# Layer 1's stick-breaking attention written out in slots of one head, and running sums of two convolutions held in PSUM

## The chip, the cores and the metric

The kernel runs on one core of a Trainium2 chip. The metric is the device time of one execution in microseconds (us). Of the kernel before there are three runs, 2133.7, 2135.2 and 2140.45 us; their median is 2135.2. A separate execution was profiled: it took 2129.01 us, of which 2127.0 us are the span that the trace covers.

## The reference

256 tokens of 1024 channels pass a first block (four mixers side by side, an output projection, an MLP) and a second block of two layers (a pooling layer and a stick-breaking attention, each followed by a PEER layer of 16384 experts). All is float32. What the change touches:

```python
def conformer_conv_mixer(u, dw_w, dw_b, gn_g, gn_b):          # 31 taps a channel
    val, gate = jnp.split(u, 2, axis=-1)
    z = val * jax.nn.sigmoid(gate)
    z = causal_depthwise_conv(z, dw_w) + dw_b
    z = group_norm_channels(z, gn_g, gn_b)
    return jax.nn.silu(z)

def rglru_mixer(u, conv_w, conv_b, wa, ba, wx, bx, lam):      # 4 taps a channel
    xr, gate = jnp.split(u, 2, axis=-1)
    xc = causal_depthwise_conv(xr, conv_w) + conv_b
    ...
    _, h = lax.associative_scan(combine, (a, bterm), axis=1)
    return (h * jax.nn.gelu(gate.astype(jnp.float32))).astype(u.dtype)

# second block, layer 1: 16 heads of 64 channels, 16 meta tokens in front of 256
q = rmsnorm(jnp.einsum('bld,de->ble', hn, w_q[j]).reshape(B, L, SB_HEADS, SB_HEAD_DIM), q_norm[j])
mix = jnp.einsum('ble,ed->bld', stick_breaking(q, k_sh, v_sh), w_o[j])
# in stick_breaking, by blocks of 128 queries
    z = jnp.einsum('bhqd,bhkd->bhqk', q_blk, kp) * scale
    valid = (key_pos[None, :] < q_pos[:, None]) & key_real[None, :]
    log_keep = jnp.where(valid, jax.nn.log_sigmoid(-z), 0.0)
    after = lax.cumsum(log_keep, axis=3, reverse=True) - log_keep
    wgt = jnp.where(valid, jnp.exp(jax.nn.log_sigmoid(z) + after), 0.0)
    return jnp.einsum('bhqk,bhkd->bqhd', wgt.astype(v.dtype), vp)
```

## The kernel before, in words

Channels lie on the 128 partitions and tokens along them, 256 tokens in the first block and 272 (L, with the meta tokens, NM = 16) in the second. Weights come as tiles of 128 x 1024 float32 through four raw buffers that SyncE's queue fills (`_Stream`). Each tile is split in two: ScalarE copies it in the reduced format to one of three `hi` buffers (line 256), and VectorE or GpSimd subtracts to get `lo` (line 267); the letters in the tables from line 357 on ("V" or "G") say which. `proj` (line 424) multiplies one tile with the activations, 16 products with `hi` (activations high and low in turn) and 8 with `lo`; `acc3` does the same for the output projections, with the sums of all 8 output tiles in four banks. PSUM has eight banks `bank[0]` to `bank[7]`. Every instruction that goes through the wrappers `T` (TensorE), `V` (VectorE), `S` (ScalarE) and `G` (GpSimd, mostly) has the line 200 in the trace, so groups are told apart by tile names and shapes; `big` is the large SBUF tile from which most work arrays are cut.

The mixers. The 20 tiles of the input projection follow one another in the order `W_ORD`. Behind each, the generators of the mixers are pulled: `conf(0)`, the 31-tap convolution of the first 128 channels, on VectorE; `conf(1)`, the second 128, with products on ScalarE and additions on GpSimd; `lru()`, the recurrent mixer, whose four taps, elementwise work and scans run on VectorE, ScalarE and GpSimd; and `att(c)`, softmax attention of 4 heads. A pull hands out an allowance in ns for each engine, from which each step takes what it yields (335 for a tap of `conf(0)`). The output projection then takes the mixers' rows in the order `K_ORD` = 4, 6, 2, 5, 7, 3, 1, 0, where 6 and 7 are the recurrent mixer's; its inputs are split into `XX` on ScalarE and VectorE. In both stages the program text is only the starting point: outside blocks under `tc.manual_schedule()` a scheduler reorders the instructions of each engine by its own model of the time.

A tap multiplies a shifted input with one weight per partition and adds the running sum, one VectorE instruction of 128 x 256:

```python
V.scalar_tensor_tensor(acc, zp[c][:, t:t + SEQ], cols[:, w0 + t:w0 + t + 1], acc, op0=ALU.mult, op1=ALU.add)
```

The attention of layer 1 (`stick`). First the 8 blocks of values are projected and turned to tokens on partitions (`v_out`), in three pieces of keys, 0 to 127, 128 to 255, and 256 to 271. `project(c)` projects one K tile and one Q tile, each holding two heads, squares them, sums the squares over a head by a product with ones (`half`), and takes the norm: for K by Ln and Exp on ScalarE, for Q by an addition on VectorE, a power on GpSimd (line 1652) and a multiplication by 0.125. `attend(c)` does two heads: scores of the first 128 queries against 144 keys and of the other 128 against 272, VectorE adds the mask, ScalarE takes Abs, Exp and Ln, VectorE adds the maximum and runs two reversed scans, GpSimd subtracts (line 1675), ScalarE takes Exp. The weights are turned by five transposes, copied to SBUF by ScalarE and VectorE, and multiplied by the values with the turned weights as TensorE's stationary operand and 64 columns of values moving; the result of two heads is copied, transposed twice, and split into `aH` and `aL`. In the text `project(c + 1)` stands ahead of `attend(c)`, and the output projection with `wo` behind all heads; the scheduler mixes them.

## Time and profile before

| | |
|---|---|
| median of three runs | 2135.2 us (2133.7 to 2140.45) |
| profiled execution, its span | 2129.01 us, 2127.0 us |
| TensorE matmuls busy | 2048.0 us, 96% of the span |
| VectorE busy | 1619.5 us, 76% |
| ScalarE busy | 1264.3 us, 59% |
| GpSimd busy | 1095.2 us, 51% |
| mean granted clock of TensorE | 0.972 |

The span is the time between the first and the last instruction in the trace, and a share is busy time by span. TensorE counts as busy while a matmul is in it, also where it runs at a lower clock, so its 96% doesn't say that it worked at full speed. The granted clock is 1.0 at 2.4 GHz and 0.5 at 1.2 GHz, and a mean between them is a mixture. In time, the input projection and the mixers lie before 131.5 us, then the MLP, the pooling layer, the first PEER layer, from 1168.84 us on the attention of layer 1, and behind it the second PEER layer.

### The profile page before, as it was taken

To read this page: it belongs to the slowest core of one execution; us is meant where nothing else is said; L and a number is where in the kernel's file an instruction comes from. 1 tells how busy PE (TensorE), PEld (TensorE's weight loads), DVE (VectorE), ACT (ScalarE), POOL (GpSimd) and SP (SyncE) were. 2 spreads that over 40 slices of the span, in tenths; PEclk is the share of its full clock that TensorE was granted. 3 is DMA by queue.
4 is the path that set the end of the run, shared out by engine and by line. 5 is a ranking of instruction groups with operands and counts; after the bars stand their busy time and mean duration, and the time that the engine had idled before them with its cause. 6 is when DMAs were issued, how large, how long until landed. Compare 5 with 4: busy or idle time off the path is not lost.

```text
span 2127.0 us, 42088 instructions
## 1 busy us (share of the span) xinstructions
PE 2048.0 (96%) x15922; PEld 1960.2 (92%) x15924; DVE 1619.5 (76%) x3169; ACT 1264.3 (59%) x2541; POOL 1095.2 (51%) x671
## 2 busy tenths in 40 slices
PE   7889999999999998999999999899999998999999
PEld 6789998999999996999999988899999997999998
DVE  7964845999688788788887484899766677877875
ACT  4654445555777785555555574455688876555554
POOL 5745836587677772333332351568776763333200
PEclk8999999999999997999999997999999998999999
DMA  5336653355676775899895521445676666889874
GB/s 187 129 111 205 210 191 102 123 190 185 207 239 210 256 239 196 312 332 345 309 316 201 164 85 54 156 135 189 197 238 218 210 209 210 309 297 330 306 251 140
DMA packets 127962, 451.54 MB, mean 212 GB/s; under 512 B 16576, under 2 KB 19776, under 8 KB 126992
## 3 DMA queue, kind: packets, MB, share of 16 engines
q1 hardware_dynamic: 100192, 352.86, 49.6%
q0 software_dynamic: 24592, 88.32, 11.3%
q10 hardware_dynamic: 2976, 7.68, 1.0%
q8 instruction: 126, 2.06, 0.4%
q14 instruction: 76, 0.62, 0.1%
HBM read 445.00 MB, written 3.67 MB: 211 GB/s over the span
## 4 chain that ended last, share of the span: by engine, by line
PE 69%; DVE 13%; issue 4%; ACT 4%; POOL 3%; DMA 1%; POOLq 0%; ACTq 0%; DVEq 0%
PE bank L200 69%; DVE big L200 9%; POOL lo L267 2%; ACT hi L256 1%; ACT oHL L200 1%; DVE bank L200 1%; DVE lo L267 1%; DVE XX L200 1%; DVE oAB L200 1%; POOL big L1257 1%; ACT big L200 1%; DMA big<-ur,sp_e 0%; DMA raw<-u 0%; DVE lo L200 0%; POOL big L943 0%
## 5 line engine op out<-in xcount | busy, mean ns | idle before, releaser
L200 PE MATMUL bank<-XX,hi 128*128 128x224 f32 (+3 forms) x7360 | 1135.0, 303 | 21.4 <-ACT hi L256 9.3
L200 PEld LDWEIGHTS bank<-XX,hi 128*128 128x128 f32 x7360 | 1001.5, 192 | 52.7 <-ACT hi L256 12.0
L256 ACT ACTIVATE hi<-raw 128x1024 fp32r<-128x1024 f32 x616 | 649.4, 1056 | 401.1 <-PE bank L200 372.5
L267 POOL TENSOR_TENSOR lo<-raw,hi 128x1024 fp32r<-128x1024 f32 x276 | 675.1, 2460 | 379.1 <-ACT hi L256 329.5
L200 PE MATMUL bank<-XX,lo 128*128 128x224 f32 (+2 forms) x4672 | 630.0, 276 | 7.2 <-POOL lo L267 5.7
L200 PEld LDWEIGHTS bank<-XX,lo 128*128 128x128 f32 x4672 | 595.0, 192 | 17.3 <-POOL lo L267 8.2
L267 DVE TENSOR_TENSOR lo<-raw,hi 128x1024 fp32r<-128x1024 f32 x340 | 433.0, 1274 | 163.8 <-ACT hi L256 144.8
L200 ACT ACTIVATE big<-bank 128x256 f32<-128x256 f32 (+33 forms) x391 | 125.1, 325 | 152.0 <-DVE big L200 79.6
L200 ACT ACTIVATE oHL<-oAB,picks 128x128 f16<-128x128 f16 x592 | 189.7, 389 | 13.3 <-DVE oAB L200 13.3
L200 DVE TENSOR_TENSOR big<-big,bank 128x256 f32<-128x256 f32 (+38 forms) x295 | 91.8, 312 | 122.1 <-ACT big L200 112.1
L200 DVE SCALAR_TENSOR_TENSOR big<-big 128x1024 f32<-128x1024 f32 (+5 forms) x89 | 117.2, 1321 | 17.9 <-DMA big<-ur,sp_e 9.1
L1257 POOL DMA_INDIRECT big<-v,sp_e x48 | 68.7, 1431 | 106.5 <-DVE big L200 103.5
L1257 POOL DMA_INDIRECT big<-ur,sp_e x56 | 79.2, 1415 | 85.7 <-DVE big L200 81.2
L200 DVE TENSOR_TENSOR oAB<-bank,picks 128x1024 f16<-128x1024 f32 (+1 forms) x112 | 114.2, 1034 | 0.0
L200 PE MATMUL bank<-big 128*128 128x128 f32 (+9 forms) x472 | 88.1, 315 | 11.4 <-ACT big L200 8.7
L200 ACT ACTIVATE XX<-big 128x224 fp32r<-128x224 f32 (+1 forms) x216 | 81.4, 377 | 28.0 <-DVE big L200 27.8
L200 PE MATMUL bank<-oHL,oAB 128*128 128x128 f16 x896 | 79.5, 226 | 15.0 <-ACT oHL L200 11.2
L200 PEld LDWEIGHTS bank<-big 128*128 128x128 f32 (+3 forms) x472 | 67.5, 197 | 24.3 <-ACT big L200 11.1
L200 DVE TENSOR_TENSOR XX<-big,XX 128x224 fp32r<-128x224 f32 (+1 forms) x214 | 86.1, 404 | 0.0
L256 ACT ACTIVATE hi<-more 128x1024 fp32r<-128x1024 f32 x48 | 50.9, 1060 | 56.8 <-PE bank L200 55.3
L200 PEld LDWEIGHTS <-oAB 128*128 128x128 f16 x896 | 55.6, 100 | 28.4 <-issue 20.9
L200 ACT ACTIVATE big<-big 128x416 f32<-128x416 f32 (+5 forms) x120 | 53.8, 469 | 45.4 <-DVE big L200 36.9
(189 smaller groups left out, 2383.3 us busy)
## 6 DMA issues: line engine op xcount, KB each, us to landing
raw<-u SPq DMA_DIRECT2D x256, 512.0 KB
raw<-v SPq DMA_DIRECT2D x208, 512.0 KB
raw<-w SPq DMA_DIRECT2D x64, 512.0 KB
more<-v SPq DMA_DIRECT2D x48, 512.0 KB
raw<-wq SPq DMA_DIRECT2D x32, 512.0 KB
raw<-win SPq DMA_DIRECT2D x16, 512.0 KB
raw<-wkv SPq DMA_DIRECT2D x16, 512.0 KB
raw<-wout SPq DMA_DIRECT2D x8, 512.0 KB
```

The costliest lines, as they stand in the source:

```text
L200: i = f(*a, **k)
L256: nc.scalar.activation(hi, raw, AF.Copy)
L267: eng.tensor_sub(self.lo[i % self.nh], raw, self.hi[i % self.nh].bitcast(F32))
L1257: nc.gpsimd.indirect_dma_start(out=dst, out_offset=None, in_=src, in_offset=bass.IndirectOffsetOnAxis(ap=at, axis=0))
```

## The change

In the mixers the running sum of `conf(0)` is kept in `bank[1]` and that of the four taps of `lru` in `bank[7]`; the last tap of each writes to SBUF. A tap of `conf(0)` now yields 400 instead of 335.

In the attention the values come in two pieces of 128 keys (the 256 tokens) and one of 16 (the meta tokens); the head's output is computed already transposed, with 64 columns of values as the stationary operand and the turned weights moving; the factor 0.125 is folded into the norm of the keys. Everything from the values on is written out in one order under `tc.manual_schedule()`: slots from -3 to 17, one head each, where the scores are of head s, the transposes of head s - 1 and the outputs of head s - 2, with one K or Q tile in each slot up to 12 and the `wo` tiles in slots 13 to 17. `mid` is the product with ones, placed between the products with `hi` and those with `lo`. The remaining helpers (`k_in`, `k_norm`, `k_out`, `q_in`, `q_norm`, `z_in`, `z_act`, `z_scan`, `z_exp`) hold the same instructions as the text before.

```diff
@@ -371,8 +371,8 @@
         for b in range(8):
             st.add(A["wkv"][8 + b], "A", "GVVVVGVV"[b])
         for b in range(8):
-            st.add(A["wkv"][b], "A", "GVVVGVVV"[b])
-            st.add(A["wsq"][b], "A", "GVVGGGGG"[b])
+            st.add(A["wkv"][b], "A", "V")
+            st.add(A["wsq"][b], "A", "G")
         for b in range(8):
             st.add(A["wo"][b], "A", "V")
         add_peer(1)
@@ -421,11 +421,12 @@
             T.matmul(out, xl, wh, start=False, stop=False)
             T.matmul(out, xh, wl, start=False, stop=last)
-        def proj(out, wt, xh, xl):
+        def proj(out, wt, xh, xl, mid=lambda: None):
             h, l = wt
             for k in range(KC):
                 T.matmul(out, h[:, k], xh[:, k], start=k == 0, stop=False)
                 T.matmul(out, h[:, k], xl[:, k], start=False, stop=False)
+            mid()
             for k in range(KC):
                 T.matmul(out, l[:, k], xh[:, k], start=False, stop=k == KC - 1)
@@ -572,11 +573,12 @@
                 w0 = COLS["conf_dw_w"] + 31 * c
                 acc = new()
                 if c == 0:
-                    V.tensor_scalar(acc, zp[c][:, 0:SEQ], cols[:, w0:w0 + 1], C("conf_dw_b", c), op0=ALU.mult, op1=ALU.add)
-                    yield (335, 0, 0)
+                    pacc = bank[1][:, 0:SEQ]
+                    V.tensor_scalar(pacc, zp[c][:, 0:SEQ], cols[:, w0:w0 + 1], C("conf_dw_b", c), op0=ALU.mult, op1=ALU.add)
+                    yield (400, 0, 0)
                     for t in range(1, 31):
-                        V.scalar_tensor_tensor(acc, zp[c][:, t:t + SEQ], cols[:, w0 + t:w0 + t + 1], acc, op0=ALU.mult, op1=ALU.add)
-                        yield (335, 0, 0)
+                        V.scalar_tensor_tensor(acc if t == 30 else pacc, zp[c][:, t:t + SEQ], cols[:, w0 + t:w0 + t + 1], pacc, op0=ALU.mult, op1=ALU.add)
+                        yield (400, 0, 0)
                 else:
                     tmp = [new() for _ in range(3)]
                     S.activation(acc, zp[c][:, 0:SEQ], AF.Identity, scale=cols[:, w0:w0 + 1], bias=C("conf_dw_b", c))
@@ -616,9 +618,10 @@
                 xc, r, ig, tau, rec, a, m = (new(2, SEQ) for _ in range(7))
                 for c in range(2):
                     w0 = COLS["lru_conv_w"] + 4 * c
-                    V.tensor_scalar(xc[:, c], xrp[c][:, 0:SEQ], cols[:, w0:w0 + 1], C("lru_conv_b", c), op0=ALU.mult, op1=ALU.add)
+                    px = bank[7][:, 0:SEQ]
+                    V.tensor_scalar(px, xrp[c][:, 0:SEQ], cols[:, w0:w0 + 1], C("lru_conv_b", c), op0=ALU.mult, op1=ALU.add)
                     for t in range(1, 4):
-                        V.scalar_tensor_tensor(xc[:, c], xrp[c][:, t:t + SEQ], cols[:, w0 + t:w0 + t + 1], xc[:, c], op0=ALU.mult, op1=ALU.add)
+                        V.scalar_tensor_tensor(xc[:, c] if t == 3 else px, xrp[c][:, t:t + SEQ], cols[:, w0 + t:w0 + t + 1], px, op0=ALU.mult, op1=ALU.add)
                         yield (400, 0, 0)
                 for c in range(2):
                     bk = bank[7]
...
-                V.tensor_scalar_mul(m[:, 16:20], m[:, 16:20], 0.125)
...
-                    T.transpose(tbk[:, 0:128], a[:, 0:128], ident)
-                    T.transpose(tbk[:, 128:256], a[:, 144:272], ident)
-                    T.transpose(tbk[:, 256:384], a[:, 272:400], ident)
-                    T.transpose(t2k[0:16, 0:128], a[:, 128:144], ident)
-                    T.transpose(t2k[0:16, 128:256], a[:, 400:416], ident)
-                    S.activation(w[:, 0:384], tbk[:, 0:384], AF.Copy)
-                    V.tensor_copy(w[0:16, 384:640], t2k[0:16, 0:256])
-                    hs = slice(64 * h, 64 * h + 64)
-                    o = [obk[:, 128 * i + 64 * hh:128 * i + 64 * hh + 64] for i in range(2)]
-                    T.matmul(o[0], w[:, 0:128], vt[0][:, hs], start=True, stop=False)
-                    T.matmul(o[0], w[0:16, 384:512], vt[1][0:16, hs], start=False, stop=True)
-                    T.matmul(o[1], w[:, 128:256], vt[0][:, hs], start=True, stop=False)
-                    T.matmul(o[1], w[:, 256:384], vt[1][:, hs], start=False, stop=False)
-                    T.matmul(o[1], w[0:16, 512:640], vt[2][0:16, hs], start=False, stop=True)
-                at = atok[c % 2]
-                S.activation(at, obk[:, 0:256], AF.Copy)
-                for i in range(2):
-                    T.transpose(obk[:, 256 + 128 * i:384 + 128 * i], at[:, 128 * i:128 * i + 128], ident)
-                S.activation(aH[:, c], obk[:, 256:512], AF.Copy)
-                V.tensor_sub(aL[:, c], obk[:, 256:512], aH[:, c].bitcast(F32))
...
-            project(0)
-            for c in range(8):
-                    project(c + 1)
-                attend(c)
-            for c in range(8):
-                h, l = st.get(1 if c == 7 else None)
...
+            def v_copy(b):
+                bk = bank[2 + b % 2]
+                S.activation(vt[:, :, 128 * b:128 * b + 128], bk[:, 0:256].rearrange("p (j d) -> p j d", j=2), AF.Copy)
+                S.activation(va[0:16, 128 * b:128 * b + 128], bk[0:16, 256:384], AF.Copy)
...
+                        V.scalar_tensor_tensor(kq, C("k_norm"), 0.125, C("q_norm"), op0=ALU.mult, op1=ALU.mult)
...
+            def k_tile(c, mid):
+                proj(kbank(c), st.get(1), XH, XL, mid)
...
+            def turn(h):
+                a = ab[h % 4]
+                T.transpose(bank[1][:, 0:128], a[:, 16:144], ident)
+                T.transpose(bank[1][:, 128:256], a[:, 160:288], ident)
+                T.transpose(bank[1][:, 256:384], a[:, 288:416], ident)
+                T.transpose(bank[2][0:16, 0:128], a[:, 0:16], ident)
+                T.transpose(bank[2][0:16, 128:256], a[:, 144:160], ident)
+            def w_copy(h):
+                w = wt_[h % 4]
+                S.activation(w[:, 0:384], bank[1][:, 0:384], AF.Copy)
+                V.tensor_copy(w[0:16, 384:640], bank[2][0:16, 0:256])
+            def o_mm(h):
+                w = wt_[h % 4]
+                o = bank[3][64 * (h % 2):64 * (h % 2) + 64, 0:256]
+                hs = slice(64 * h, 64 * h + 64)
+                T.matmul(o, vt[:, 0, hs], w[:, 0:256], start=True, stop=False)
+                T.matmul(o[:, 128:256], vt[:, 1, hs], w[:, 256:384], start=False, stop=False)
+                T.matmul(o, va[0:16, hs], w[0:16, 384:640], start=False, stop=True)
+            def o_out(c):
+                S.activation(aH[:, c], bank[3][:, 0:256], AF.Copy)
+                V.tensor_sub(aL[:, c], bank[3][:, 0:256], aH[:, c].bitcast(F32))
...
+                for s in range(-3, 18):
+                    live = 0 <= s < 16
+                    for i in {-3: (4, 5), -2: (6, 7)}.get(s, ()):
+                        v_copy(i)
+                    for i in (6, 7) if s == -3 else ():
+                        v_mul(i)
+                    if 0 <= s - 2 < 16:
+                        w_copy(s - 2)
+                    kc = (s + 2) // 2 if s % 2 == 0 and s < 13 else None
+                    qc = kd = (s + 1) // 2 if s % 2 and 0 < s + 1 < 15 or s == -1 else None
+                    mid = lambda: None
+                    if kc is not None:
+                        k_in(kc)
+                    if qc is not None:
+                        q_in(qc)
+                    if 0 <= s - 1 < 16:
+                        z_exp(s - 1)
+                    if kc is not None:
+                        S.activation(s_k[kc % 2], kr[kc % 2], AF.Square)
+                        mid = lambda: k_mm(kc)
+                    if qc is not None:
+                        S.activation(s_q[qc % 2], qr[qc % 3], AF.Square)
+                        mid = lambda: q_mm(qc)
+                    if live:
+                        z_mm(s)
+                    if 0 <= s - 2 < 16:
+                        o_mm(s - 2)
+                    if live:
+                        z_in(s)
+                        z_act(s)
+                    if s < 13:
+                        if st.ln < st.hn:
+                            st.split_l()
+                        st.split_h()
+                    if live:
+                        z_scan(s)
+                    if kd is not None:
+                        k_norm(kd)
+                        k_out(kd)
+                    if s % 2 and 0 <= s - 2 < 16:
+                        o_out((s - 2) // 2)
+                    if s < 13:
+                        (k_tile if s % 2 else q_tile)((s + 3) // 2, mid)
+                    elif qc is not None:
+                        mid()
+                    if qc is not None:
+                        q_norm(qc)
+                    if 13 <= s < 17:
+                        wo_tile()
+                        if s in (14, 16):
+                            wo_tile()
+                    if s == 17:
+                        wo_tile()
+                        wo_tile()
+                    for i in (6, 7) if s == -3 else ():
+                        v_turn(i)
+                    if 0 <= s - 1 < 16:
+                        turn(s - 1)
```

On TensorE, late in the heads of layer 1 (bank_61 to bank_68 are `bank[0]` to `bank[7]`, `sqh`, `sql` and `XX` are activations, `hi_` and `lo_` the buffers of split tiles), these rows stood before:

```order
L200 MATMUL bank_65<-big 128x64 x10
L200 MATMUL bank_64<-ident,big 128x128 x3
L200 MATMUL bank_63<-ident,big 16x128 x2
L200 MATMUL bank_66<-half,big 128x2
L200 MATMUL bank_67<-big 128x144
L200 MATMUL bank_67<-big 128x272
L200 MATMUL bank_61<-big 128x144
L200 MATMUL bank_61<-big 128x272
L200 MATMUL bank_68<-aH,hi_74 128x256
L200 MATMUL bank_68<-aL,hi_74 128x256
```

And these stand there now, from the scores of a head to the transposes that end its slot:

```order
L200 MATMUL bank_61<-big 128x144
L200 MATMUL bank_61<-big 128x272
L200 MATMUL bank_64<-big 64x256
L200 MATMUL bank_64<-big 64x128
L200 MATMUL bank_64<-big 64x256
L200 MATMUL bank_65<-XX,hi_75 128x272 x16
L200 MATMUL bank_63<-half,big 128x2 x2
L200 MATMUL bank_65<-XX,lo_78 128x272 x8
L200 MATMUL bank_62<-ident,big 128x128 x3
L200 MATMUL bank_63<-ident,big 16x128 x2
```

The ten products of 64 columns for two heads are now three products of 256, 128 and 256 columns for one, the tile is whole but for the two products with ones inside it, and no output projection stands among the heads here.

On VectorE, at the end of the mixers, before (the two SCALAR_TENSOR_TENSOR of 128x256 from `big` alone are the recurrent mixer's scans, `XX<-yT,XX` the inputs of the output projection):

```order
L200 TENSOR_SCALAR big<-big 128x2
L200 SCALAR_TENSOR_TENSOR big<-big 128x256 x2
L200 TENSOR_SCALAR big<-big,cols 128x256
L200 TENSOR_SCALAR big<-bank_62 128x4
L267 TENSOR_TENSOR lo_77<-raw_71,hi_74 128x1024
L200 TENSOR_TENSOR XX<-yT,XX 128x256 x2
L200 SCALAR_TENSOR_TENSOR big<-big,cols 128x256
```

And now:

```order
L267 TENSOR_TENSOR lo_77<-raw_71,hi_74 128x1024
L200 TENSOR_TENSOR XX<-yT,XX 128x256
L200 SCALAR_TENSOR_TENSOR big<-big,cols 128x256
L200 TENSOR_TENSOR XX<-yT,XX 128x256
L200 TENSOR_SCALAR big<-big 128x128
L200 TENSOR_SCALAR big<-big 128x256
L200 TENSOR_TENSOR big<-big,bank_61 128x256
L200 SCALAR_TENSOR_TENSOR big<-big 128x256 x2
L200 COPY big<-big 128x256
```

The two scans stood in front of the first inputs of the output projection and a split (`lo_77`), and stand behind that split and the first two inputs now.

## Rows read from the trace of the kernel before

**Rows 1.** Page, part 4: the chain that ended last, share by engine.

```profile
PE 69%; DVE 13%; issue 4%; ACT 4%; POOL 3%; DMA 1%; POOLq 0%; ACTq 0%; DVEq 0%
```

**Rows 2.** Windows: length, busy PE, PEld, DVE, ACT, POOL (count), clock, DMA share, GB/s.

```profile
30.70:131.50 100.80, 89.01 (x638) 81.51 (x637) 86.98 (x135) 56.33 (x104) 66.95 (x59) 0.93 0.40 133
1168.84:1270.00 101.16, 99.91 (x746) 91.65 (x744) 67.30 (x124) 65.82 (x136) 42.75 (x25) 1.00 0.39 126
1270.00:1320.00 50.00, 49.92 (x249) 42.74 (x249) 25.52 (x55) 24.08 (x51) 10.72 (x10) 0.69 0.03 11
```

**Rows 3.** VectorE groups, 28 to 120 us: busy us, mean ns, idle before.

```profile
L200 DVE SCALAR_TENSOR_TENSOR big<-big,cols 128x256 f32<-128x256 f32 x40 | 34.2, 866 | 0.5
...
L200 DVE TENSOR_TENSOR big<-bank,rb 128x256 f32<-128x256 f32 x14 | 5.6, 409 | 0.0
```

**Rows 4.** VectorE in time: start, length in us, instruction.

```profile
51.11 2.36 DVE L200 SCALAR_TENSOR_TENSOR big<-big,cols 128x256 f32<-128x256 f32 x1
...
53.92 0.47 DVE L200 SCALAR_TENSOR_TENSOR big<-big,cols 128x256 f32<-128x256 f32 x1
```

**Rows 5.** VectorE groups, whole span.

```profile
L200 DVE TENSOR_TENSOR big<-bank,big 128x400 f32<-128x400 f32 x66 | 37.9, 575 | 2.6
L200 DVE TENSOR_TENSOR bank<-bank,big 128x400 f32<-128x400 f32 x66 | 37.8, 573 | 0.0
```

**Rows 6.** Waits of PE, 30 to 112 us: total us, times, longest.

```profile
PE bank L200 <- DVE big L200: 8.4, 5, 2.8
```

**Rows 7.** PE in time, mixers: start, length, matmuls (xcount).

```profile
46.46 3.18 PE L200 MATMUL bank<-XX,hi 128*128 128x256 f32 x15
...
63.34 0.87 PE L200 MATMUL bank<-big 128*64 128x256 f32 x4 [0.37 <-ACT big L200]
```

**Rows 8.** PE in time, values of layer 1.

```profile
1168.84 2.16 PE L200 MATMUL bank<-XX,hi 128*128 128x272 f32 x16
1170.85 1.15 PE L200 MATMUL bank<-XX,lo 128*128 128x272 f32 x8
```

**Rows 9.** PE in time, heads of layer 1.

```profile
1253.31 0.97 PE L200 MATMUL bank<-big 64*128 64x144 f32 x4
...
1255.15 3.31 PE L200 MATMUL bank<-big 128*128 128x64 f32 x20
1258.39 0.77 PE L200 MATMUL bank<-ident,big 128*128 128x128 f32 x5
```

**Rows 10.** VectorE groups, 1160 to 1332 us.

```profile
L267 DVE TENSOR_TENSOR lo<-raw,hi 128x1024 fp32r<-128x1024 f32 x22 | 27.5, 1256 | 18.6 <-ACT hi L256 13.0 <-PE bank L200 2.8 <-issue 2.7
L200 DVE SCALAR_TENSOR_TENSOR big<-big 128x416 f32<-128x416 f32 x16 | 12.5, 782 | 3.7 <-ACT big L200 3.6
L200 DVE TENSOR_TENSOR_SCAN big<-big 128x272 f32<-128x272 f32 x16 | 11.1, 694 | 0.0
L200 DVE SCALAR_TENSOR_TENSOR big<-bank,big 128x272 f32<-128x272 f32 x16 | 7.8, 488 | 0.0
...
L200 DVE TENSOR_TENSOR_SCAN big<-big 128x144 f32<-128x144 f32 x16 | 7.2, 447 | 0.1
...
L200 DVE SCALAR_TENSOR_TENSOR big<-big 128x272 f32<-128x272 f32 x8 | 6.5, 817 | 4.9 <-ACT big L200 4.9
...
L200 DVE SCALAR_TENSOR_TENSOR big<-bank,big 128x144 f32<-128x144 f32 x16 | 5.8, 362 | 3.2 <-PE bank L200 2.6 <-ACT big L200 0.4
```

**Rows 11.** ScalarE groups, the same stretch.

```profile
L200 ACT ACTIVATE big<-big 128x416 f32<-128x416 f32 x48 | 25.7, 546 | 18.5 <-DVE big L200 10.1 <-POOL big L1675 8.0
L200 ACT ACTIVATE big<-big,misc 128x416 f32<-128x416 f32 x16 | 10.2, 635 | 0.1
```

**Rows 12.** GpSimd groups, the same stretch.

```profile
L1675 POOL TENSOR_TENSOR big<-big 128x416 f32<-128x416 f32 x16 | 21.2, 1325 | 43.5 <-DVE big L200 38.6 <-ACT big L200 4.9
L1652 POOL TENSOR_TENSOR big<-big,misc 128x4 f32<-128x4 f32 x8 | 8.6, 1071 | 12.2 <-DVE big L200 12.2
```

**Rows 13.** Tile aH: length min/median/max in ns, first and last start in us.

```profile
L200 PE MATMUL bank<-aH,hi x64: 276/281/582, 1275.4 to 1336.9; 128*128 128x256 f32 x64
```

More of the change, by code (lines that the diff above doesn't have):

```diff
@@ L1581, in stick @@
             onesr = fl(L)
[L1582 removed]
             kq = fl(1)
[L1584 to L1618 removed]
+            va = fl(D)
+            vt = fl(2, D)
+            vT = [fl(L) for _ in range(4)]
             kn = [fl(L) for _ in range(3)]
@@ new lines, in kbank, with k_in, k_mm, k_norm @@
+            def kbank(c):
+                return bank[4 if c else 7][:, 0:L]
+            def k_tile(c, mid):
+                proj(kbank(c), st.get(1), XH, XL, mid)
+            def k_in(c):
+                V.tensor_mul(kr[c % 2], kbank(c), rb)
+            def k_mm(c):
+                T.matmul(bank[6][:, 0:L], half[:, 0:P], s_k[c % 2], start=True, stop=True)
+            def k_norm(c):
+                S.activation(s_k[c % 2], bank[6][:, 0:L], AF.Ln, bias=eps)
+                S.activation(s_k[c % 2], s_k[c % 2], AF.Exp, scale=-0.5)
@@ new lines, in k_out, with q_tile, q_in, q_mm @@
+            def k_out(c):
+                V.scalar_tensor_tensor(kn[c % 3], kr[c % 2], kq, s_k[c % 2], op0=ALU.mult, op1=ALU.mult)
+            def q_tile(c, mid):
+                proj(bank[5][:, 0:SEQ], st.get(1), qh, ql, mid)
+            def q_in(c):
+                V.tensor_mul(qr[c % 3], bank[5][:, 0:SEQ], rb[:, NM:L])
+            def q_mm(c):
+                for j, (a, e, r) in enumerate(TILES[SEQ]):
+                    T.matmul(bank[2][:, 256 + 2 * j:258 + 2 * j], s_q[c % 2][:, a:e], half[:, 128:130], start=True, stop=True)
@@ new lines, in q_norm, with z_mm @@
+            def q_norm(c):
+                m = sm[c % 3]
+                V.tensor_scalar_add(m[:, 0:4], bank[2][:, 256:260], EPS)
+                G.tensor_tensor(m[:, 16:20], m[:, 0:4], mhalf[:, 0:4], op=ALU.pow)
+            def z_mm(h):
+                pb = slice(64 * (h % 2), 64 * (h % 2) + 64)
+                k, q = kn[h // 2 % 3], qr[h // 2 % 3]
+                T.matmul(bank[0][:, 0:144], q[pb, 0:128], k[pb, 0:144], start=True, stop=True)
+                T.matmul(bank[0][:, 144:416], q[pb, 128:256], k[pb, 0:272], start=True, stop=True)
@@ new lines, in z_in, with z_act @@
+            def z_in(h):
+                z, m, hh = zb[h % 4], sm[h // 2 % 3], h % 2
+                V.scalar_tensor_tensor(z[:, 0:144], bank[0][:, 0:144], m[:, 16 + hh:17 + hh], mask[:, 128:272], op0=ALU.mult, op1=ALU.add)
+                V.scalar_tensor_tensor(z[:, 144:416], bank[0][:, 144:416], m[:, 18 + hh:19 + hh], mask, op0=ALU.mult, op1=ALU.add)
+            def z_act(h):
+                z, a = zb[h % 4], ab[h % 4]
+                S.activation(a, z, AF.Abs)
+                S.activation(a, a, AF.Exp, scale=-1.0)
+                S.activation(a, a, AF.Ln, bias=one)
@@ new lines, in z_scan, with z_exp @@
+            def z_scan(h):
+                z, a, r = zb[h % 4], ab[h % 4], rv[h % 4]
+                V.scalar_tensor_tensor(a, z, 0.0, a, op0=ALU.max, op1=ALU.add)
+                for s0, s1 in ((0, 144), (144, 416)):
+                    V.tensor_tensor_scan(r[:, s0:s1][:, ::-1], onesr[:, 0:s1 - s0], a[:, s0:s1][:, ::-1], 0.0, op0=ALU.mult, op1=ALU.add)
+                G.tensor_sub(z, z, r)
+            def z_exp(h):
+                S.activation(ab[h % 4], zb[h % 4], AF.Exp)
+            def turn(h):
[5 more added lines that the diff above has]
+                T.transpose(bank[2][0:16, 128:256], a[:, 144:160], ident)
```

120 lines of the change are left out of this document (44 added, 76 removed).

## The prediction

> **What bounds the kernel now.** I read the chain of waits first, then a table by stage, then inside the two stages that the change touches the groups of instructions and the order in time. The chain [rows 1] says 69% TensorE and 13% VectorE: mostly the matmuls themselves set the end, and VectorE at a few places. The stages tell where. In the mixers (30.7 to 131.5 us) TensorE is busy for 89.0 of 100.8 us at a granted clock of 0.93; VectorE for 87.0. In the attention of layer 1, TensorE has no gap: 99.91 of 101.16 us, then 49.92 of 50.00, but in the second stretch at a clock of 0.69 [rows 2]. So the mixers can gain by taking time from VectorE, the attention only by fewer or cheaper matmuls, or by a better clock. A stage that is faster ends earlier and shifts everything behind it, since what follows (the MLP, the second PEER) streams weights through the same four buffers as before.
>
> **The change part by part: mixers.** 30 taps of the 31-tap convolution and 6 of the 8 taps of the recurrent mixer lose one of two SBUF operands: the running sum is read from a PSUM bank and written back there, the last tap to SBUF. Four of the 40 instructions in the group (the short convolution) stay. The group's mean is 866 ns [rows 3]. One that runs undisturbed took 0.47 us, one some microseconds earlier 2.36 [rows 4]: same operands, same shape, so the difference is a neighbour. It isn't PSUM traffic: in the same stretch the products that read a bank and one SBUF tile keep to 409 ns [rows 3], while GpSimd is busy for 67 of 101 us [rows 2]. I read it as two SBUF operands against GpSimd, and that the new form escapes it. What the tap itself costs with source and destination in the same bank isn't in the trace; nearest are additions of 400 columns, 573 ns in place in a bank against 575 from bank to SBUF [rows 5]. So in place costs nothing extra there, and a tap should take 0.47: 36 x (0.866 - 0.47) = 14.2 us less VectorE time. The other end: if reading and writing one bank took two passes, the tap would cost about 0.47 + 0.27 (256 columns more, at the 0.575 / 400 us a column of rows 5 less its fixed part, taken as a quarter), and 36 x 0.13 = 4.6 us would be left.
>
> The Trainium skill (Perfetto Trace Analysis, "Optimizing Scalar/DVE Operations") gives VectorE about 60 ns of access overhead on SBUF and about 125 on PSUM. By it every converted tap would be 65 ns dearer, 36 x 0.065 = 2.3 us, and 11.9 instead of 14.2 would be saved. Rows 5 show no such difference for the destination (573 against 575), so I do not subtract it.
>
> How much of 14.2 reaches the end? TensorE waited 8.4 us for VectorE here, in five waits [rows 6], and behind a wait it ran slowly: the 15 products from 46.46 took 3.18 us, 0.2 each, where 0.125 is usual later [rows 7, 8]. The clock of 0.93 over 89 us of work is another 89.0 x 0.07 = 6.2 us. TensorE can thus gain 8.4 + 6.2 = 14.6 at most. Against it, the order of the program has changed: the two scans of the recurrent mixer now stand among the last VectorE instructions of the stage, behind two of the inputs of the output projection, where they stood in front of all of them; a tap counts 400 instead of 335 in the budget that a projection grants, so fewer taps go beside each. The output projection takes the recurrent mixer second, so a late scan is a wait there. I take three quarters of 8.4 and half of 6.2: 9 us. Bounds: 0 (the scans arrive as late as now) and 14.
>
> **Attention: matmuls.** A projected tile is 16 products from 1168.84 to 1170.85 and 8 in 1.0 after it, 3.0 us, 0.125 each; of 256 columns instead of 272, 2.8 [rows 8]. (A record's length overlaps the next one's start by about 0.15, which I take off everywhere.) Outputs cost 20 records in 3.31 us for two heads, 1.65 a head [rows 9]. The new form has the values as 64-column weights and the turned attention weights streaming: six records a head. Layer 0's head output has the same form, four records in 0.87, 0.2 each [rows 7]: 6 x 0.2 = 1.2, saving 0.45 x 16 = 7.2 us. Its result is already transposed, so 16 records of transposes go (five take 0.65 [rows 9]): 2.1 us. With them go 8 copies on ScalarE, and 8 tiny multiplications on VectorE; neither engine is the limit there, so I count these at nothing for the end but as air in the loop below.
>
> The stage now runs from 1168.84 to 1337.2 (last product of the output projection at 1336.9 plus 0.28 [rows 13]), 168.4 us. A mean clock of 0.69 over 50 us means 62% of it at the lower level, 31 us, which do the work of 15.5. At full clock the work is 168.4 - 15.5 = 152.9, and with the change 152.9 - 7.2 - 2.1 = 143.6. That is the floor of the new stage.
>
> **Attention: the loop.** The order is now written out by slots, one head each; in a slot TensorE does scores 0.9, outputs 1.2, a tile 2.9, a ones-product 0.3, turns 0.65 [rows 8, 9]: 5.95 us. Against it stands a serial loop over two slots: scores in (0.49 + 0.36), ScalarE's three (2 x 0.546 + 0.635 = 1.73), VectorE's softplus and scans (0.78 + 0.69 + 0.45 = 1.92), GpSimd's subtraction 1.33, the exponential 0.55, a square of at most 0.5, then 1.73 and 1.92 of the next head, K's norm 0.82 and the power 1.07 that the scores of the next pair need [rows 10 to 12]. Sum 12.4, or 6.2 a slot: 0.25 over TensorE, 4 us over 16 slots. In the last slots a split of 1.26 on VectorE [rows 10] stands ahead of the copy that the outputs wait for, twice or so: 2.5 us. 143.6 + 4 + 2.5 = 150.1, so 18 us are gained, of which 9 are matmuls and 9 the clock, since the output projection that ran between waits in the slow stretch now fills slots 13 to 17. Bounds: 24 (no loop, no stall), and 2.5 if the slow stretch comes back elsewhere with its 15.5 us.
>
> The rest I cost at nothing: the lower halves of the K tiles all on VectorE and of the Q tiles all on GpSimd (as many on each as before); the factor 0.125 folded into the key norm; ones-products between the two halves of a tile, which move a wait to where 16 products stand in front of it; the value blocks copied in two pieces instead of three, hidden behind six tiles of 3.0. If the cover fails, each such wait is a few tenths.
>
> **Sum.** 9 + 18 = 27 us. The profiled execution took 2129.0 (span 2127.0 and 2.0 around it), so 2102 for it; the median of the runs is 6.2 higher, 2135.2, so 2108.
>
> **Rivals.**
> - Mixers give nothing: taps in one bank are no faster, or the late scans eat it. For it: the scans' new place; against: 409 and 573 ns in rows 3 and 5. 2108 + 9 = 2117.
> - Both parts reach their bounds (14 and 24): 2135 - 38 = 2097. For it: VectorE is the only engine that TensorE waits for over 2 us in the mixers; against: the loop is over TensorE by its rows.
> - The loop is longer: each hand-over between engines costs something that the rows' lengths don't hold. Ten hand-overs at 0.2 more give 14.4, 7.2 a slot, 16 x 1.0 = 16 us, and the attention gives 2: 2124. For it: TensorE's order is fixed now and has nothing to put into a wait, where the old order mixed products of tiles between heads.
> - Slower: TensorE falls to its lower clock level inside the slots. It did so here at 1270 [rows 2] and after a wait at 46 us [rows 7]. A short wait in every slot, which the loop predicts, could hold it there: 5.95 x 0.2 / 0.125 = 9.5 us a slot instead of 6.2, 3.3 more. Over 16 slots that is 53, 2161; from 8 slots on it eats the 27, from 10 the kernel is measurably slower. Against it: from 1168 to 1270 the clock is 1.00 with the same heads.
> - The change does not act: taps are as disturbed as before, the slots as slow: 2135.
>
> **How the numbers follow.** Forecast 0.52 (own range 2101 to 2116), mixers nothing 0.15, both bounds 0.11, longer loop 0.08, low clock 0.09, no effect 0.05. About 0.3%, 6.4 us, is what a measurement of this kernel tells from no change: below 2128.8 or above 2141.6. Faster: 0.52 + 0.15 + 0.11 and most of the longer loop, 0.83. Within 0.3%: 0.07, the no-effect case and a loop still longer. Slower: 0.10. The range 2095 to 2128 holds the forecast, the mixers' rival, most of the bounds' and most of the longer loop's; the low clock and no effect lie outside.
>
> **What would show it.** In the changed kernel's groups, a group of taps from and to a bank with 470 to 500 ns (right), or 700 and more (wrong). Waits of TensorE for VectorE before 112 us of 3 us or less, and an end of the output projection near 122 instead of 131.5. In the attention, output records of 0.2 us, slots 6.0 to 6.4 us apart, a granted clock of 0.95 or more through all slots, and the last product of the output projection about 27 us earlier. Slots of 7 and more with the waits on scores show the longer loop; 9 and more at a clock near 0.5 the slower side. The prediction is wrong if the end comes no earlier by the sum of the two stages, that is if the later stages take the gain back.

## The result and the profile after

The changed kernel takes 2109.78 us (median of 4 runs, 2108.21 to 2110.99), the kernel before 2134.99 beside it; the ratio is 0.9889 with a 95% interval of 0.9867 to 0.9912, so 19 to 28 us less. In a second set the ratio was 0.9887 (0.9869 to 0.9905). The prediction was 2108. The profiled execution of the changed kernel took 2109.76 us, with a span of 2107.9 us and a mean granted clock of 0.977.

Single executions mislead by some microseconds, and not because of anything that was changed. A statistics product sums the squares that a norm needs; one stands right behind the mixers, one near the start of the attention. These are the two in two of the runs told below (start, length, instruction); nothing between them differs in the code. First c2:

```profile
123.56 1.95 PE L200 MATMUL bank<-misc,big 128*128 128x1 f32 x16
...
1159.16 1.39 PE L200 MATMUL bank<-misc,big 128*128 128x1 f32 x12
```

Then b1:

```profile
123.31 1.95 PE L200 MATMUL bank<-misc,big 128*128 128x1 f32 x16
...
1169.04 1.39 PE L200 MATMUL bank<-misc,big 128*128 128x1 f32 x12
```

1035.6 against 1045.7 us for the same work. So the two changed stages are compared below by their own lengths in the traces, and whole kernels by their ratios. The mixers are counted from the fifth tile of their projection (30.70 us before, 30.53 after) to the statistics product behind them, the attention from the statistics product in it to the end of its last product with `aH` and `lo`.

After, the stages by window (columns as in [rows 2]): mixers; values and the slots up to 1; the end of slot 1, and slot 2; slots 3 to 12; slots 13 to 17.

```profile
30.53:122.95 92.42, 85.76 (x654) 80.21 (x652) 76.03 (x136) 60.00 (x108) 66.35 (x59) 0.96 0.46 151
1159.79:1201.50 41.71, 41.64 (x330) 40.11 (x329) 20.09 (x39) 23.92 (x50) 12.73 (x7) 1.00 0.43 139
1201.50:1213.57 12.07, 9.99 (x46) 7.63 (x44) 6.53 (x13) 5.71 (x11) 5.72 (x4) 0.72 0.27 89
1213.57:1278.47 64.90, 64.32 (x421) 49.72 (x420) 42.17 (x90) 46.58 (x86) 25.71 (x19) 1.00 0.25 82
1278.47:1317.10 38.63, 36.39 (x260) 30.11 (x259) 24.11 (x37) 20.36 (x34) 9.12 (x7) 1.00 0.36 124
```

In the mixers VectorE is busy for 76.0 us in this window, instead of 87.0 in that of [rows 2]. The statistics product behind the mixers, before and after:

```profile
133.71 1.95 PE L200 MATMUL bank<-misc,big 128*128 128x1 f32 x16
```

```profile
123.18 1.95 PE L200 MATMUL bank<-misc,big 128*128 128x1 f32 x16
```

The stage takes 92.65 us instead of 103.01, which is 10.4 less. The 131.5 us at which [rows 2], the account of the profile before and the prediction end the mixers is too early: the products of the output projection go on to 133.6. The taps after, by group, VectorE, 20 to 120 us (busy us, mean ns, idle before):

```profile
L200 DVE SCALAR_TENSOR_TENSOR bank<-big,cols,bank 128x256 f32<-128x256 f32 x33 | 15.4, 481 | 0.3
...
L200 DVE SCALAR_TENSOR_TENSOR big<-big,cols 128x256 f32<-128x256 f32 x4 | 2.9, 714 | 0.0
```

A tap in PSUM takes 481 ns, against 866 [rows 3]; the four of the short convolution, still with two SBUF operands, take 714. GpSimd is as busy as before (66.35 us). What TensorE waited for there (wait in us, times, longest), and the place:

```profile
PE bank L200 <- DVE big L200: 5.3, 2, 4.9
```

```profile
95.00 1.22 PE L200 MATMUL bank<-ident,big 128*128 128x128 f32 x4 [4.89 <-DVE big L200]
```

8.4 us in five waits [rows 6] have become 5.3 in two, and nearly all of that is one wait. The four records behind it spread the factors of a group norm; the copy that they wait for runs on VectorE from 93.60 to 94.95 us. The last tap of `conf(0)` was over at 72.9, so this isn't a wait for the taps.

In the attention, two slots of after in time, the first with a K tile, the second with a Q tile and shortened by the middle rows of its tile:

```profile
1213.57 2.33 PE L200 MATMUL bank<-big 64*128 64x144 f32 x10
1215.84 2.27 PE L200 MATMUL bank<-XX,hi 128*128 128x272 f32 x16
1217.94 0.50 PE L200 MATMUL bank<-half,big 128*128 128x2 f32 x4
1218.31 1.24 PE L200 MATMUL bank<-XX,lo 128*128 128x272 f32 x8
1219.38 0.99 PE L200 MATMUL bank<-ident,big 128*128 128x128 f32 x5
1220.31 2.33 PE L200 MATMUL bank<-big 64*128 64x144 f32 x10
...
1225.91 0.71 PE L200 MATMUL bank<-ident,big 128*128 128x128 f32 x5
1226.55 2.33 PE L200 MATMUL bank<-big 64*128 64x144 f32 x10
```

The ten records that begin a slot are the scores (4) and the outputs (6), 2.27 us from start to start. Two slots last 1226.55 - 1213.57 = 12.98 us, and no row shows a wait, yet the same five transposes take 0.93 in the first slot (to 1220.31) and 0.64 in the second: a short wait can hide inside a group. The attention ends at 1316.8 + 0.28 instead of 1337.1 + 0.28; from the statistics product it is 154.3 us instead of 165.6:

```profile
1162.79 1.39 PE L200 MATMUL bank<-misc,big 128*128 128x1 f32 x12
```

```profile
L200 PE MATMUL bank<-aH,lo x64: 276/281/384, 1283.6 to 1316.8; 128*128 128x256 f32 x64
```

And of before:

```profile
1171.83 1.39 PE L200 MATMUL bank<-misc,big 128*128 128x1 f32 x12
```

```profile
L200 PE MATMUL bank<-aH,lo x64: 276/281/516, 1276.4 to 1337.1; 128*128 128x256 f32 x64
```

### The profile page after: what moved, and what is told of

Read it like the earlier page. It is cut to its first block, busy times and chain, and to the rows that moved or that the text cites. A ratio compares the mean times of both kernels' runs of the same rounds, so it can differ in the third digit from the quotient of the medians.

```text
span 2107.9 us, 41888 instructions
## 1 busy us (share of the span) xinstructions
PE 2030.8 (96%) x15844; PEld 1935.8 (92%) x15844; DVE 1597.7 (76%) x3161; ACT 1267.3 (60%) x2526; POOL 1090.1 (52%) x671
## 4 chain that ended last, share of the span: by engine, by line
PE 70%; DVE 14%; ACT 6%; issue 4%; POOL 4%; DMA 1%; POOLq 0%; SPq 0%; ACTq 0%; DVEq 0%
PE bank L200 70%; DVE big L200 10%; POOL lo L267 2%; ACT big L200 2%; ACT hi L256 2%; ACT oHL L200 1%; DMA big<-ur,sp_e 1%; DVE lo L267 1%; DVE XX L200 1%; DVE bank L200 1%; POOL big L588 1%; DVE oAB L200 1%; POOL big L1260 1%; POOL big L946 0%; DVE lo L200 0%
## 5 line engine op out<-in xcount | busy, mean ns | idle before, releaser
L200 ACT ACTIVATE big<-bank 128x224 f32<-128x224 f32 (+40 forms) x375 | 120.7, 327 | 156.2 <-DVE big L200 76.6
L200 ACT ACTIVATE oHL<-oAB,picks 128x128 f16<-128x128 f16 x592 | 189.9, 390 | 15.7 <-DVE oAB L200 15.5
L200 DVE SCALAR_TENSOR_TENSOR big<-big 128x1024 f32<-128x1024 f32 (+5 forms) x89 | 109.5, 1233 | 36.1 <-ACT big L200 25.5
L200 PE MATMUL bank<-big 128*128 128x128 f32 (+9 forms) x408 | 78.7, 320 | 11.1 <-ACT big L200 9.3
L200 PEld LDWEIGHTS bank<-big 128*128 128x128 f32 (+3 forms) x408 | 51.4, 175 | 29.4 <-ACT big L200 14.8
L267 DVE TENSOR_TENSOR lo<-more,hi 128x1024 fp32r<-128x1024 f32 x48 | 58.7, 1223 | 25.1 <-ACT hi L256 25.1
```

The source lines that it names most:

```text
L200: i = f(*a, **k)
L267: eng.tensor_sub(self.lo[i % self.nh], raw, self.hi[i % self.nh].bitcast(F32))
```

## The experiments

**The two parts, each alone.** a1 is the changed kernel again. a2 is before with the taps in PSUM, a3 is after with the taps in SBUF. The line of a tap, with `w` for the slice of the weight:

```diff
-V.scalar_tensor_tensor(acc, zp[c][:, t:t + SEQ], w, acc, ...)
+V.scalar_tensor_tensor(acc if t == 30 else pacc, zp[c][:, t:t + SEQ], w, pacc, ...)
```

> The changed kernel once more, as the yardstick of this set. Its profiled execution was 19 us shorter than that of before, its runs 25 us. If the larger figure is the change, the ratio here is 0.988 again; if the runs of before happened to be slow, it moves towards 0.991.

> Before, with only the running sums of the mixers in PSUM. Theory (the two parts act apart): the output projection of the mixers ends at about 123 us instead of 131.5 and the whole is 9 us shorter. Rival (the gain in the mixers is given back later, because later stages wait for the stream of weights): stage 9 us shorter, whole 0 to 4.

> After, with the taps in SBUF again. Theory: the mixers end at 131.5 us as before, the attention takes 157 us instead of 168, and the whole is 11 us shorter (by the prediction 18). Rival: the attention gains 18 by itself and lost 7 only because the stage came earlier; then 18.

a1 2110.97 us, 0.9887. a2 2119.48, 0.9946 (0.9928 to 0.9965): 11.5 us. a3 2122.52, 0.9948 (0.9930 to 0.9966): 11.1 us. Within the noise they add up to the change, and both rivals fall: the mixers' part is not given back later (it is 10.5 us in its stage in a2), and the attention's is 11 and not 18 also when it stands alone. Its stage takes 155.5 us in a3 and 165.8 in a2; in a1, which is the changed kernel again, it takes 155.7, so lengths of one stage can differ by 1.4 us without a cause in the code.

**The new outputs without the slots (a4).** Before, with values in two pieces and one of 16, three products a head and no second transposes; the scheduler orders them:

```diff
-T.matmul(o[0], w[:, 0:128], vt[0][:, hs], start=True, stop=False)
-...
+o = obk[64 * hh:64 * hh + 64, 0:256]
+T.matmul(o, vt[:, 0, hs], w[:, 0:256], start=True, stop=False)
+T.matmul(o[:, 128:256], vt[:, 1, hs], w[:, 256:384], start=False, stop=False)
+T.matmul(o, va[0:16, hs], w[0:16, 384:640], start=False, stop=True)
```

> Before, with only the new form of the head outputs (values as stationary operand, three products a head, keys in text order, no second transposes), left to the scheduler's order. Theory (the new form takes work from TensorE, and the order decides the clock): 4 to 7 us shorter, the granted clock in the last 60 us of the attention still under 0.8. Rival (the slow stretch came from the old outputs' waits): the clock rises to 1 and 12 us or more are gained without any slots.

2115.49 us, 0.9920 (0.9902 to 0.9938): 17 us, by the medians more than the whole attention part of the change, though the intervals of a3 and a4 overlap. The rival's numbers came out; its cause, waits of the old outputs, isn't shown: in the slow stretch of before TensorE was busy for 49.92 of 50.00 us [rows 2]. The windows of a4:

```profile
1167.00:1270.00 103.00, 103.00 (x726) 87.55 (x724) 68.23 (x129) 67.96 (x132) 41.03 (x26) 1.00 0.35 117
1270.00:1300.00 30.00, 30.00 (x199) 23.56 (x199) 22.62 (x44) 18.30 (x35) 9.53 (x7) 1.00 0.16 53
1300.00:1318.30 18.30, 18.30 (x139) 15.57 (x137) 9.17 (x14) 8.57 (x14) 4.45 (x3) 1.00 0.60 201
```

TensorE is busy without a gap at a granted clock of 1.00 to the end. Where before had 0.69 [rows 2], the scheduler's order with the new products has no slow stretch at all, although it still places the output projection among the heads. The stage:

```profile
1170.84 1.39 PE L200 MATMUL bank<-misc,big 128*128 128x1 f32 x12
```

```profile
L200 PE MATMUL bank<-aH,lo x64: 276/278/387, 1280.8 to 1318.0; 128*128 128x256 f32 x64
```

147.4 us, 18 less than before and 7 to 8 less than with the slots (154.3 to 155.7). This comparison of stages is clear of the 1.4 us by which equal code differs.

**The change without its slots (b1, c3, c2).** b1 is a4 with the taps in PSUM. c3 is b1 with the factor 0.125 folded into K's norm and the low halves divided as in the change. c2 is b1 with a tap at 335 in the pull's budget.

```diff
-V.tensor_scalar_mul(m[:, 16:20], m[:, 16:20], 0.125)          # c3
-yield (400, 0, 0)                                              # c2
+yield (335, 0, 0)
```

> Before, with the taps in PSUM and the new form of the head outputs, and the scheduler's order kept in the attention: the change without its slots. The two alone gave ratios 0.9946 and 0.9920. Theory (they add, and the slots cost something): 0.987, or 2105 us, 5 us less than the changed kernel; attention stage 149 us. Rival (the slots are worth something once the stage comes earlier): no faster than the changed kernel, 2110.

> The same version with the factor 0.125 folded into the norm of K, all low halves of the K tiles on VectorE and all of the Q tiles on GpSimd: the change without the slots. The prediction costs these edits at nothing: 2103, within 2 us. Rival: the eight multiplications of 0.9 us on VectorE were in the way, 3 us or more faster.

> The version with the taps in PSUM and the new outputs in the scheduler's order, with a tap at 335 in the pull's budget instead of 400. Theory (the budget decides how late the convolution ends, and TensorE's one long wait in the mixers, 4.9 us at 90 us, is for its end): the wait is 1 to 3 us shorter and the kernel 1 to 3 us faster, 2101. Rival (the scheduler evens that out): no change, 2103.

b1 2103.36 us, 0.9859 (0.9839 to 0.9880); c3 2106.89, 0.9866 (0.9841 to 0.9891); c2 2107.87, 0.9880 (0.9857 to 0.9903). The attention takes 147.4, 147.0 and 147.4 us in the three, so the theory of b1 holds in its stage. The whole kernels are 2 to 6 us ahead of the changed one by their medians, but each interval overlaps its own, so for the whole kernel a loss by the slots is likely and not shown. Behind the attention 3 us go back: from its end to the end of the span it is 794 us in b1 and c3 and 791 in after; why is open. By the ratios c3 is 1.5 us behind b1, so the other edits are worth nothing that shows, as predicted. In c2 TensorE's long wait is the same 4.89 us, so the budget of a tap isn't its cause.

**Inside the slots.** In after, TensorE waits for VectorE at the end of slot 1, the second with scores, and the clock falls behind that wait. TensorE of after, and then VectorE:

```profile
1201.29 0.49 PE L200 MATMUL bank<-ident,big 128*128 128x128 f32 x3
1203.85 0.39 PE L200 MATMUL bank<-ident,big 128*16 128x128 f32 x2 [2.08 <-DVE big L200]
1204.17 2.71 PE L200 MATMUL bank<-big 64*128 64x144 f32 x10
```

```profile
1203.22 0.50 DVE L200 SCALAR_TENSOR_TENSOR big<-big 128x272 f32<-128x272 f32 x1
1203.64 0.16 DVE L200 TENSOR_SCALAR big<-bank 128x4 f32<-128x4 f32 x1
```

The transposes write the bank from which VectorE still has to read Q's sums (1203.64), and that instruction stands behind the scans and K's norm (1203.22). b2 moves K's norm to the start of its slot and gives Q's sums `bank[7]`:

```diff
-T.matmul(bank[2][:, 256 + 2 * j:258 + 2 * j], s_q[c % 2][:, a:e], half[:, 128:130], ...)
+T.matmul(bank[7][:, 2 * j:2 + 2 * j], s_q[c % 2][:, a:e], half[:, 128:130], ...)
```

> After, with the norm of K taken at the start of its slot instead of the end, and the squares' sums of Q in a bank of their own. Theory (the slots lose about 8 us to hidden waits: 2.1 us in the second slot and the low clock behind it, and 0.3 in each K slot where a transpose shares its bank with the sums that VectorE reads late): the wait at 1201 and the slow tile behind it go, K slots 0.3 us shorter, 5 to 8 us less. Rival (a loop over two slots is the limit at 13 us): the waits move to the scores and the slots stay 6.5 us apart.

2106.09 us, 0.9873 (0.9853 to 0.9894): some 3 us less than after by the ratios, within the intervals, and not the 5 to 8 of the theory. TensorE of b2:

```profile
1222.30 2.33 PE L200 MATMUL bank<-big 64*128 64x144 f32 x10
...
1229.90 1.41 PE L200 MATMUL bank<-big 128*64 128x256 f32 x6 [0.19 <-DVE big L200]
...
1235.22 2.33 PE L200 MATMUL bank<-big 64*128 64x144 f32 x10
...
1278.10 1.01 PE L200 MATMUL bank<-half,big 128*128 128x2 f32 x4 [1.51 <-ACT big L200]
```

The slow tile at 1204 is gone, but the slots stay at 12.92 us for two with the wait now in front of the outputs, and a new wait of 1.51 stands in slot 13, with the low clock behind it (0.79 from 1274 to 1290). The rival described the slots better than the theory, though the wait moved to the outputs and not to the scores.

b3 puts the old outputs into the slots (ten products of 64 columns, a copy and two transposes for two heads). c4 takes the products with ones out of the tile and puts them behind it:

```diff
-            mid()
             for k in range(KC):
                 T.matmul(out, l[:, k], xh[:, k], start=False, stop=k == KC - 1)
+            mid()
```

> After, with the old form of the outputs (ten products of 64 columns for two heads and two transposes more) inside the slots. If the new form is worth what its rows say when TensorE is the limit (0.3 to 0.5 us a head and 0.3 a pair), the attention is 7 to 10 us longer. If the slots are limited by the loop, 0 to 3. If the low clock of the kernel before came from the old outputs, the clock falls here as well and it is 15 us or more.

> After, with the product with ones behind a whole tile instead of between its two halves. Theory (the slots are held by the loop at 13.0 us for two, with TensorE's own work at 12.7): the sums arrive 1.1 us later, the norm that the next scores wait for as well, and as much of it as is not covered comes on top, 0 to 0.5 us a slot, up to 6 us. Rival (TensorE alone holds them): the two switches between kinds of product that are saved make the slots 0.1 to 0.2 us shorter, 2 us faster.

b3: 2120.07 us, 0.9935 (0.9916 to 0.9953), about 10 us more than after. Its slots 3 to 12 are 13.52 us for two, without a wait in any row, at full clock; behind them the clock falls:

```profile
1227.45 2.64 PE L200 MATMUL bank<-big 64*128 64x144 f32 x14
...
1240.97 2.64 PE L200 MATMUL bank<-big 64*128 64x144 f32 x14
```

```profile
1213.00:1281.00 68.00, 68.00 (x475) 58.93 (x475) 42.15 (x90) 47.58 (x90) 25.56 (x19) 1.00 0.24 78
1281.00:1328.50 47.50, 43.38 (x291) 39.29 (x289) 24.44 (x38) 21.58 (x37) 9.38 (x7) 0.89 0.35 111
```

So TensorE is the limit in slots 3 to 12 of b3, and there the old products don't lower the clock. In slots 13 to 17 it is 0.89, where after has 1.00, and TensorE has 4.1 us of gaps instead of 2.2. Of the 12.6 us by which the stage is longer than in after (166.9 instead of 154.3), 8 lie in these last slots and under 3 in slots 3 to 12. b3 also has nearly everything of the change but its outputs, and its stage is no shorter than that of a2 (165.8): the slots alone gain nothing. c4: 2107.33 us, 0.9884 (0.9860 to 0.9908), no difference. Its slots:

```profile
1226.48 2.34 PE L200 MATMUL bank<-big 64*128 64x144 f32 x10
...
1232.89 0.39 PE L200 MATMUL bank<-ident,big 128*16 128x128 f32 x2 [0.16 <-DVE big L200]
...
1239.42 2.34 PE L200 MATMUL bank<-big 64*128 64x144 f32 x10
```

12.94 for two: TensorE saves its switches and waits 0.16 instead, now in a row of its own. Neither side had that. Three different orders inside the slots give 12.92 to 12.98, with 0.2 to 0.3 of waiting in each: what they have in common is a loop over two slots of 12.9 to 13.0 us, and TensorE's own work is only 0.2 to 0.3 below it. Which step of the loop decides isn't shown.

**What holds up a tap (b4).** Before, with the GpSimd additions of the second half of the convolution left out:

```diff
-G.tensor_add(acc, acc, tmp[t % 3])
```

> Before, without the 30 additions on GpSimd of the second half of the convolution (its sum is left out, so the output is not the reference's). Theory (a tap with two SBUF operands is held up by GpSimd): the taps, still in SBUF, fall from 866 ns to below 650, those left long standing beside the other GpSimd work. Rival (a sum that is read and written in SBUF is slow by itself): they stay at 800 or more.

One execution of b4 took 2124.53 us. The mean of its 40 taps is 773 ns, between the two. The rows in time decide. VectorE of b4, and then GpSimd:

```profile
41.19 2.58 DVE L200 SCALAR_TENSOR_TENSOR big<-big,cols 128x256 f32<-128x256 f32 x1
...
49.22 2.54 DVE L200 SCALAR_TENSOR_TENSOR big<-big,cols 128x256 f32<-128x256 f32 x1
...
54.40 0.47 DVE L200 SCALAR_TENSOR_TENSOR big<-big,cols 128x256 f32<-128x256 f32 x1
```

```profile
40.20 3.29 POOL L267 TENSOR_TENSOR lo<-raw,hi 128x1024 fp32r<-128x1024 f32 x1 [2.31 <-ACT hi L256]
49.09 2.39 POOL L267 TENSOR_TENSOR lo<-raw,hi 128x1024 fp32r<-128x1024 f32 x1 [5.60 <-ACT hi L256]
66.49 2.50 POOL L267 TENSOR_TENSOR lo<-raw,hi 128x1024 fp32r<-128x1024 f32 x1 [15.01 <-ACT hi L256]
```

From 51.48 to 66.49 GpSimd does nothing, and each tap there takes 0.47 to 0.49; a tap that meets a split of GpSimd lasts until the split is over, or 0.3 us longer. A sum kept in SBUF is not slow by itself. The expected figure was too low because five such splits, at 2 us of waiting each, were left. So of the 0.40 us by which a mean tap of before exceeds 0.47, the 30 additions account for 0.09 only; 0.30 are still there without them, most of it from the splits.

**Wider old products (c1).** Before, with 128 columns of values in each old output product:

```diff
-o = [obk[:, 128 * i + 64 * hh:128 * i + 64 * hh + 64] for i in range(2)]
+hs = slice(128 * c, 128 * c + 128)
+o = [obk[:, 256 * hh + 128 * i:256 * hh + 128 * i + 128] for i in range(2)]
```

> Before, with each of the old output products streaming 128 columns of values instead of 64 (both heads' values, of which one half is used): as many products, twice the columns, and one copy more on ScalarE for two heads. Theory (the lower clock level in the last third of the attention came with the runs of 64-column products): the granted clock from 100 us after the start of the attention is over 0.9 instead of 0.7, and the kernel is 5 to 12 us faster though it computes more. Rival (the fall has to do with the order and the waits, not with the width): the clock stays at 0.7, and the kernel is 0 to 8 us slower.

2138.13 us, 1.0019 (1.0003 to 1.0035). The same stretch as in [rows 2]:

```profile
1270.00:1320.00 50.00, 47.03 (x275) 37.76 (x275) 29.82 (x60) 28.80 (x58) 10.96 (x10) 0.86 0.12 39
```

The clock lies between the two figures, but the copy added and a shared bank brought gaps that before doesn't have (TensorE is busy for 47.03 us here and for 49.92 there), so it decides nothing.

## Why the prediction was right, point by point

**The taps** were sized rightly: 0.47 forecast, 481 ns measured. The rows for the mechanism are b4's: a tap with two SBUF operands took 2.54 to 2.58 us beside a subtraction on GpSimd and 0.47 to 0.49 while GpSimd was idle. The Trainium skill says so (SBUF — State Buffer, "Who interferes with whom": a VectorE instruction with two SBUF inputs contends with a GpSimd instruction that reads SBUF, one with at most one, outside the modes that use both ports, does not), and these rows agree. The dearer access to PSUM that the Trainium skill gives (Perfetto Trace Analysis, "Optimizing Scalar/DVE Operations") doesn't show: 481 in PSUM, 0.47 to 0.48 undisturbed in SBUF.

**The mixers** were put at 9 us; they gave 10.4 in their stage, and 11.5 in the whole kernel (a2). The bound of 14 held, and the late scans did not decide. The split was less good. Waits for VectorE were to give 6.3 and gave 3.1 (8.4 less 5.3), since one wait of 4.9 us is left that the prediction did not see as one. The clock was to give 3.1 and gave about 2.8 (0.93 to 0.96). The other 4.5 us stand in neither term.

**The attention** was put at 18 us and gave 11 (a3): this is the term that was mis-sized. As the prediction counts, from the first row of [rows 8] to the last product of the output projection, the stage was to take 150.1 us: 143.6 of work on TensorE at full clock, 4 for the loop, 2.5 in the last slots. It takes 157.3 (1159.79 to 1317.1). The windows of after split this: TensorE has 5.0 us of gaps, the clock of 0.72 over 12.07 us costs 3.4, and 148.9 are left as work and short hidden waits. So two steps failed.

- The matmuls. The floor of 143.6 was 5 to 7 us too low. a4 shows it best: with the new products, no gap and a clock of 1.00 it takes 150.4 by this count, where the prediction put the old products at 152.9 at full clock. So they save at most 2.5 us and not 9.3. A head's six records take 1.37 us (2.27 less 0.9 for the scores) and not 1.2, and the sixteen transposes less are not seen in the total. In the slots a head's work on TensorE is some 6.4 us where 5.95 was summed.
- The start of the slots, to which no cost was given. It has a wait of 2.08 us, and the low clock behind it.

The two terms for waiting were nearer: 6.5 forecast, 5.0 measured, with slots 6.49 apart instead of 6.2 and waits of 0.36 to 0.93 in the last ones. That a4 without any slots comes out at the 150.1 that was forecast with them is chance, since it has none of these waits and more work.

The clock did come back, and its 15.5 us are the larger part of what a4 gains. But "9 the clock, since the output projection [...] now fills slots 13 to 17" isn't borne out as the cause: a4 has the projection among the heads at a clock of 1.00, and b3 has it in slots 13 to 17 at 0.89. In these last slots the clock went with the new products and not with the place of the projection; whether the products themselves do it, or the order that the scheduler gives them, a4 doesn't separate. What the slots add is a loss of 7 to 8 us in the stage, against a4: the gaps of 5.0 and the slow stretch of 3.4.

**The sum** of 27 came out as 24 to 25. That 2108 lies within 2 us of the result is partly luck: the mixers gave 1 to 3 more than forecast, the attention 7 less, and the profiled pair differs by 19.1 us only.

**The signs.** The taps came out as named. TensorE's waits for VectorE fell to 5.3 and not to 3, the slots are 6.49 apart and not 6.0 to 6.4, the clock wasn't 0.95 or more in all of them, and the last output product came 20.3 us earlier in the profiled pair and not 27.

**The rivals.** The longer loop was named and priced at 7.2 a slot; it is 6.5. The low clock inside the slots came once, at the start, and not in all slots.

What stays open is why TensorE fell to the lower level at 1270 us in the kernel before. It had just done 20 records of 64 columns in a row and went on without a gap:

```profile
1267.57 3.40 PE L200 MATMUL bank<-big 128*128 128x64 f32 x20
1270.90 1.25 PE L200 MATMUL bank<-ident,big 128*128 128x128 f32 x5
```

The five transposes behind it took 1.25 us. But the same 20 records at 1255.15, with transposes of 0.77 behind them [rows 9], left the clock at 1.00, so such a run isn't enough by itself. In b3 the same products, ten records at a time, left it at 1.00 in slots 3 to 12; it was lower in front of them and behind them, where TensorE has gaps.

## What to carry to other kernels

Before an order is written out by hand, give the new instructions to the old order: here the new products alone were worth 17 us, most of it by the clock, and the hand-written order made their stage 7 to 8 us longer again. When VectorE works beside a busy GpSimd, look in time at its slow instructions of one shape; here they ended when a GpSimd instruction ended, and one operand in PSUM freed them. Where a loop is within a few tenths of the busiest engine's work, as here, moving one wait gained little: it turned up in front of the next instruction.

## What the runs showed of the hardware that was not expected

- A 128 x 256 tap with two SBUF operands takes 0.47 us, and 2.54 to 2.58 beside a GpSimd subtraction of 128 x 1024. With the sum in a bank it takes 481 ns, source and destination being the same bank.
- An untouched stretch of the program, between the mixers and the attention, took 1035.6 to 1045.7 us in different profiled executions.
- A product of 16 keys by 64 columns with 256 moving columns isn't cheaper than one of 128 keys. TensorE of after, in slot 16, where a wait separates the two kinds:

```profile
1300.64 0.87 PE L200 MATMUL bank<-big 128*64 128x256 f32 x4 [0.36 <-ACT big L200]
1302.43 0.64 PE L200 MATMUL bank<-big 16*64 16x256 f32 x2 [0.93 <-DVE big L200]
1303.00 0.38 PE L200 MATMUL bank<-aH,hi 128*128 128x256 f32 x1
```

The four records of 128 keys, two with 256 moving columns and two with 128, take 0.87, or 0.2 each; the two of 16 keys take 0.57 to the next start, or 0.29 each.
